# Hybrid streaming encoder step: second part of each weight tile by accumulating DMA instead of GpSimd, and its products after all those with first parts

## The chip, the core and the metric

The kernel runs on one core of a Trainium2 chip. The core has TensorE (PE in the profile; its weight loads are the row PEld), VectorE (DVE), ScalarE (ACT), GpSimd (POOL) and SyncE (SP), each with its own queue of instructions that run in order, and 16 DMA engines. Engines wait for each other through semaphores. The metric is the device time of one execution in microseconds (us); lower is better.

## The reference, cut to what matters

One layer of a hybrid encoder runs over 512 prompt tokens and 64 sample tokens (576 columns together):

```python
shift, scale, gate = split(silu(c) @ W_ada + b_ada, 3)
h = rmsnorm(x, norm_w) * (1 + scale) + shift
proj = h @ W_in                                  # 2048 -> 18032 columns
y_a = (gated RMSNorm of gated_delta_rule(conv(qkv))) @ W_bA   # 16 heads, chunks of 64
y_b = (sparse_attention(top-k of indexer scores) * silu(z)) @ W_bB
x = x + gate * ((sigmoid(ga) * y_a + sigmoid(gb) * y_b) @ W_out)
return final_rmsnorm(x), new caches, new states
```

The four large products (W_in, W_bA, W_bB, W_out) fill most of the time. All data are float32.

## The kernel before, in words

**The main stream.** The weights are cut into 189 tiles of 128 output columns (2048 x 128, held as 128 partitions x 2048 elements, 1 MB): 141 of W_in and 16 each of W_bA, W_bB and W_out. A tile multiplies the 576 columns of activations in two halves of 288. TensorE multiplies in float32r, which keeps fewer bits than float32, so each operand is split in two: for weights, `whi` is the tile rounded to float32r (ACT, a copy) and `wlo` is tile minus `whi` (GpSimd, a subtraction); activations are split in the same way (`hh` and `hl`; later `ga`, `gb`, `mg`). For each of 16 blocks of rows, `half` (line 285) issues three products: whi x high, whi x low, wlo x high. That makes 48 products per half and 96 per tile.

**Buffers.** The raw tile `wraw`, `whi` and `wlo` have two buffers each. While tile n is multiplied, `run_tile` (line 301) has tile n+1 split in four quarters of 128 x 512, one after each of products 4, 14, 24 and 34 of the first half (`split`, line 273), and has tile n+3 loaded after product 10 of the second half, product 58 of the tile (`load`, line 261, from SP). That load goes into the raw buffer of tile n+1, so it waits until that tile is split. Each half of the result has a PSUM bank out of three (`pm`), read by an epilogue (`epi`) on ACT and DVE as soon as the half ends.

**Order of the rest.** Convolutions, delta rule (a chain per head: convolution, decays `e`, products `kk` and `kq`, a triangular solve by the steps `Mt` and `M` on DVE, small DMAs through DRAM, the scan `px`, `pS`, `po`), indexer, top-k and attention are tasks: generators whose steps are put between the products when a rough clock in the kernel (`Plan`, lines 67 to 203) says that their inputs are there. The clock knows fixed costs for each engine's instructions and nothing of what else happens on the chip. The queues of all engines are written in that order, so an engine that comes late makes those that wait for it stand still with all that is queued behind. `join` (line 162) and `drain` emit what is left of a task without products around it.

**Stages.** Up to about 140 us the modulation weights `wa` stream in and the first two tiles are multiplied as `h` appears (`start`, with its own splits); then the indexer, and from about 450 to 1800 us the 16 heads of the delta rule; attention until about 2430 us; then the branch and output products until the end, with little else beside them. Most instructions of DVE, ACT and GpSimd are recorded by one helper, line 55, so the profile is read by tile names.

Of the kernel before, what the change touches and what calls it, by code (L numbers as in the profile page):

```python
# [7 lines left out]
F32 = mybir.dt.float32  # L8
# [9 lines left out]
KO = 16  # L18
# [16 lines left out]
def chunk(c):  # L35
    """a chunk's tokens: their number, where they begin in a sequence with the sample's history, and in one without"""
    return (128, 128 * c, 128 * c) if c < 4 else (TS, TP + 3, TP)


def by_chunk(x):  # L40
    """the prompt's chunks of a [128, 576] tile"""
    return x[:, :TP].rearrange("p (a b) -> p a b", b=128)


class Eng:
    """an engine whose instructions are also put on the plan's clock"""
# [20 lines left out]
class Plan:  # L67
    """Emission order: a main stream of matrix products, and tasks (generators) whose steps are
    emitted between its instructions when, by a rough clock, their inputs are there."""
# [92 lines left out]
    def join(self, *ts):  # L162
        """emit the rest of these tasks (and what else is due meanwhile)"""
        while any(not t.done for t in ts):
            due = min(t.due for t in self.tasks)
            if due > self.pe:
                self.pe = due
            self.tick()


# [1 line left out]
    def bank(self, pool, key, n, name, count=1):  # L172
        """PSUM banks, when the readers of what was in them should be through"""
        while True:
            u = self.banks.setdefault(key, [])
            at = max([0.0] + [self.last.get(x, 0.0) for x in u[-n:][:count]]) if len(u) >= n else 0.0
            if at <= self.pe:
                break
            yield at - self.pe
        t = [pool.tile([128, 512], F32, tag=key, name=f"{name}_{x}") for x in range(count)]  # L180
        u += [x.name for x in t]
        return t[0] if count == 1 else t
# [23 lines left out]
class Kern(Plan):  # L206
# [29 lines left out]
    def rsqrt(self, pool, x, shape, tag):  # L236
        """1/sqrt(x): bit-level start, then three Newton steps."""
        V = self.V
        v = pool.tile(shape, I32, tag=tag + "v", name=tag + "v")
        t = pool.tile(shape, F32, tag=tag + "t", name=tag + "t")  # L240
        V.tensor_scalar(v, x.bitcast(I32), 1, None, op0=ALU.logical_shift_right)
        V.tensor_scalar(v, v, -1.0, 1597463007.0, op0=ALU.mult, op1=ALU.add)
        y = v.bitcast(F32)
        for _ in range(3):
            V.tensor_tensor(t, y, y, op=ALU.mult)
            V.scalar_tensor_tensor(t, t, -0.5, x, op0=ALU.mult, op1=ALU.mult)
            V.scalar_tensor_tensor(y, t, 1.5, y, op0=ALU.add, op1=ALU.mult)
        return y
# [24 lines left out]
    def split(self, n, q, of=4, eng=None):  # L273
        if n >= len(self.stream):
            return
        d = self.stream[n]
        if q == 0:
            d["hi"] = self.wp.tile([128, 2048], F32R, tag="whi", name=f"whi{n}")
            d["lo"] = self.wp.tile([128, 2048], F32R, tag="wlo", name=f"wlo{n}")
        w = KO * d["m"] // of  # L280
        s = slice(w * q, w * q + w)
        self.A.activation(d["hi"][:, s], d["raw"][:, s], AF.Copy)
        (eng or self.G).tensor_tensor(d["lo"][:, s], d["raw"][:, s], d["hi"][:, s].bitcast(F32), op=ALU.subtract)

    def half(self, n, s, ps, ks, hook=None):
# [7 lines left out]
        for k in ks:  # L293
            for w, x in ((hi, ah), (hi, al), (lo, ah)):
                self.mm(ps[:m, :288], w[:, k, :], x[:, k, sl], start=k == 0 and i % 3 == 0, stop=k == KO - 1 and i % 3 == 2)
                i += 1
                if hook:
                    hook(i)
                self.tick()

    def run_tile(self, n):
# [4 lines left out]
        def hook0(i):  # L306
            if i in (4, 14, 24, 34):
                self.split(n + 1, (i - 4) // 10)

        def hook1(i):  # L310
            if i == 10:
                self.load(n + 3)

        for s in range(2):
            ps = self.pm.tile([128, 512], F32, tag="mm", name=f"mm{n}_{s}")
            self.half(n, s, ps, range(KO), hook1 if s else hook0)
            d["epi"](ps, s)

    def run_last(self, n):
        """the last two tiles, the first halves of both before the second ones"""  # L320
        hook = lambda i: self.split(n + 1, (i - 4) // 10) if i in (4, 14, 24, 34) else None
        for s in range(2):
            for t in (n, n + 1):
                ps = self.pm.tile([128, 512], F32, tag="mm", name=f"mm{t}_{s}")
                self.half(t, s, ps, range(KO), hook if (t, s) == (n, 0) else None)
                self.stream[t]["epi"](ps, s)

# [31 lines left out]
    def now(self, gen):  # L359
        """run a generator that needs no waiting for"""  # L360
# [25 lines left out]
    def small_vectors(self, pool, rows):  # L386
# [6 lines left out]
        # half of the taps' weights: silu(y) = (tanh(y/2) + 1) * (y/2)  # L393
# [10 lines left out]
    def c_vectors(self, pool, cr):  # L404
# [9 lines left out]
        # as stationary operands of a quarter of the array's columns  # L414
# [8 lines left out]
    def start(self, ctx, hctx):  # L423
        """shift and scale, h = modulated norm of x by feature, both in two f32r parts, as the weights
        of the modulation stream in; and the first products as h appears"""
# [7 lines left out]
        with tc.tile_pool(name="x0", bufs=2, side="right", reuse_waits="tile") as xp:  # L433
# [4 lines left out]
            def load(m):  # L438
                """two chunks of the weights"""
# [10 lines left out]
            for t in range(5):  # L450
                # the sample's tokens twice, for the halves of the features
# [45 lines left out]
            def fin(g, w):  # L497
                """the sums as [128, 4, 2 (prompt, sample)], with the bias"""
# [65 lines left out]
            def chunks():  # L564
                """the waiting chunks, each on its columns of the array"""
# [71 lines left out]
    def misc(self):  # L637
# [3 lines left out]
        # the indexer's keys in two parts, on both halves of the partitions: prompt, past, sample  # L641
# [21 lines left out]
        # indexer weights by token; for the sample also on the upper partitions  # L663
# [4 lines left out]
        # beta, g, and sums of g along the chunks  # L668
# [16 lines left out]
        # log1p(e) = e * ln(u) / (u - 1) with u = 1 + e rounded; e where u == 1  # L685
# [95 lines left out]
    def qi_epi(self, m):  # L781
        def epi(ps, s):
# [4 lines left out]
            # two heads in two parts, a part on either half of the partitions  # L787
# [64 lines left out]
    def topk(self, a, k, name):  # L852
        """the k largest of each row become MARK (of equal values the first), then the row a mask"""
# [78 lines left out]
    def tokens(self, st, nm, src, s):  # L932
        """src by token, times a scalar per token"""
# [17 lines left out]
    def decays(self, st):  # L951
        """between the tokens of a chunk, for both orientations"""
# [24 lines left out]
    def within(self, name, k, x, dst):  # L977
        """products of k with x inside the chunks, times dst"""
# [10 lines left out]
    def front_k(self, st):  # L989
# [4 lines left out]
        # |k|^2 is the diagonal  # L994
# [23 lines left out]
    def front_q(self, st):  # L1018
# [16 lines left out]
        # q with the decay from the chunk's start, and the chunks' whole decays  # L1035
# [8 lines left out]
    def solve(self, st):  # L1044
        """inverses of the chunks' unit lower triangles I - N (transposed): of the 32 x 32 blocks on their
        diagonals a system per partition, then products for the blocks below of twice the size"""
# [45 lines left out]
        # the 32 x 32 blocks, those of the first halves also not transposed  # L1092
# [20 lines left out]
        # the 64 x 64 blocks  # L1113
# [17 lines left out]
    def scan(self, st):  # L1131
# [46 lines left out]
        # norm over the head, back to features, its weight (and the half of silu(z))  # L1178
# [50 lines left out]
    def bias_setup(self):  # L1229
        """the relative bias of each head by distance, in DRAM; its far value by partition"""  # L1230
# [17 lines left out]
        # every row repeated: a row stride one short of the period then shifts by one per partition  # L1248
# [3 lines left out]
    def toeplitz(self, h, n, w):  # L1252
        """[n, w]: bias at distance c - 128 - p"""
# [47 lines left out]
    def attend_block(self, a, t, BT):  # L1301
        """128 of the prompt's queries of a head"""
# [28 lines left out]
    def softmax(self, L, mask, name, tag):  # L1331
        """L + mask to probabilities along the rows"""
# [89 lines left out]
    def silu2(self, ps, s, dst):  # L1422
        """2 silu of a PSUM half into its part of dst [128, 576]"""
# [37 lines left out]
    def gate_vectors(self):  # L1461
        """half of the third part of silu(c) @ w_ada + b_ada: sums along k by partition, then over partitions"""
# [141 lines left out]
    def out_cols(self, j, g, ts):  # L1604
        """the columns of x plus the output product, their squares' sums, and then times the final weight"""
# [24 lines left out]
    def finish(self, ts, *after):  # L1630
        """the final norm of some rows; the last columns still lack the weight"""
# [189 lines left out]
def shape_constants():  # L1821
    """arrays that depend on shapes alone: identity, chunk triangles, masks, relative-position buckets"""
# [53 lines left out]
```

## Time and profile before

| | |
|---|---|
| Times of three runs | 3176.89, 3191.1, 3197.2 us; median 3191.1 us |
| Profiled execution: span from first to last instruction | 3196.7 us (no other time of it is given; 5.6 us over the median) |
| PE busy | 3018.8 us (94%) |
| DVE, ACT, POOL busy | 1687.6 (53%), 1074.6 (34%), 1098.7 us (34%) |
| DMA | 355.20 MB, queue q1 of SP busy 39.1% of 16 engines' span |

A busy share says how long an engine had an instruction in work, not that it advanced: an instruction that is held up while it runs counts as busy. PEclk is the clock that TensorE was granted as a share of 2.4 GHz; its two levels are 1.0 and 0.5 (1.2 GHz). The DMA share is the mean busy share of the 16 DMA engines.

### The profile page before, as it was taken

What the parts mean: (1) busy time and instruction counts of PE and PEld (TensorE: products, weight loads), DVE (VectorE), ACT (ScalarE), POOL (GpSimd) and SP (SyncE); (2) the same over time, 40 slices, a digit from 0 to 9 for tenths busy, and PEclk for the clock granted to TensorE, in tenths of its full rate; (3) what the DMA queues carried; (4) which work ended last, traced back from release to release, by engine and by line L of the source; (5) the groups of instructions that cost most, each with busy time, mean ns of one, the idle gap of its engine ahead of it and who ended that gap; (6) DMA issues with size and microseconds to landing.
All of it is one profiled execution on the core that took longest, in us unless ns stands there. A gap on an engine that the chain in (4) does not pass through costs nothing.

```text
span 3196.7 us, 55681 instructions
## 1 busy us (share of the span) xinstructions
PE 3018.8 (94%) x22363; PEld 2852.4 (89%) x22363; DVE 1687.6 (53%) x4057; ACT 1074.6 (34%) x2580; POOL 1098.7 (34%) x1103
## 2 busy tenths in 40 slices
PE   6999999999999999999999989999999999999998
PEld 2688999888888888888888879999999999999997
DVE  3355998767678777777776245445442311122112
ACT  2244222343433433334333233323333322122333
POOL 2033343333333333333323323333323434444432
PEclk8999999999999999899989999999999999999999
DMA  9722333322323232232223543343334755444522
GB/s 357 229 56 60 107 98 84 89 79 76 86 77 97 80 87 66 69 89 79 75 71 93 122 121 108 95 138 107 95 100 120 202 166 154 128 136 133 152 80 86
DMA packets 513092, 355.20 MB, mean 111 GB/s; under 512 B 47489, under 2 KB 460050, under 8 KB 511618
## 3 DMA queue, kind: packets, MB, share of 16 engines
q1 hardware_dynamic: 512690, 351.58, 39.1%
q8 instruction: 176, 2.88, 0.4%
q14 instruction: 82, 0.67, 0.1%
q10 hardware_dynamic: 144, 0.07, 0.0%
HBM read 303.54 MB, written 48.04 MB: 110 GB/s over the span
## 4 chain that ended last, share of the span: by engine, by line
PE 68%; DVE 23%; DMA 3%; ACT 2%; issue 2%; SPq 1%; POOL 1%; DVEq 0%; ACTq 0%; POOLq 0%
PE mm L218 55%; DVE Mt L55 5%; DVE M L55 4%; DVE cv L55 3%; DVE L L55 2%; PE dot L218 1%; SPq L55 1%; PE ada L218 1%; PE ob L218 1%; PE lg L218 1%; PE mmp L218 1%; DVE rkt L55 1%; DMA wa<-in_w_ada 1%; POOL wlo L55 1%; DVE e L55 1%
## 5 line engine op out<-in xcount | busy, mean ns | idle before, releaser
L55 POOL TENSOR_TENSOR wlo<-wraw,whi 128x512 fp32r<-128x512 f32 x752 | 1028.3, 1388 | 2006.0 <-ACT whi L55 1898.6
L218 PE MATMUL mm<-hl,whi 128*128 128x288 f32 (+1 forms) x4448 | 1359.6, 306 | 0.0
L218 PE MATMUL mm<-hh,wlo 128*128 128x288 f32 (+1 forms) x4448 | 1356.0, 305 | 0.0
L218 PE MATMUL mm<-hh,whi 128*128 128x288 f32 (+1 forms) x4448 | 1349.2, 303 | 0.3 <-ACT kvTk L55 0.3
L218 PEld LDWEIGHTS mm<-hh,wlo 128*128 128x128 f32 (+1 forms) x4448 | 855.8, 192 | 14.9 <-issue 8.6
L218 PEld LDWEIGHTS mm<-hl,whi 128*128 128x128 f32 (+1 forms) x4448 | 855.4, 192 | 12.6 <-issue 6.2
L218 PEld LDWEIGHTS mm<-hh,whi 128*128 128x128 f32 (+1 forms) x4448 | 855.8, 192 | 9.3 <-issue 4.9
L55 ACT ACTIVATE whi<-wraw 128x512 fp32r<-128x512 f32 x756 | 433.7, 620 | 297.1 <-issue 205.2
L55 DVE TENSOR_TENSOR Mt<-M 18x30 f32<-18x30 f32 (+14 forms) x480 | 220.8, 460 | 9.1 <-issue 0.3
L55 DVE TENSOR_TENSOR M<-M,Mt 18x30 f32<-18x30 f32 (+14 forms) x480 | 205.1, 427 | 16.5
L218 PE MATMUL mm<-mg,whi 128*128 128x288 f32 x1024 | 204.5, 295 | 0.0
L218 PE MATMUL mm<-gb,whi 128*128 128x288 f32 x1024 | 204.0, 296 | 0.0
L218 PE MATMUL mm<-ga,whi 128*128 128x288 f32 x1024 | 203.5, 294 | 0.0
L218 PEld LDWEIGHTS mm<-mg,whi 128*128 128x128 f32 x1024 | 164.0, 188 | 0.0
L218 PEld LDWEIGHTS mm<-ga,whi 128*128 128x128 f32 x1024 | 164.0, 188 | 0.0
L55 DVE SCALAR_TENSOR_TENSOR cv<-raw,cw,cv 128x579 f32<-128x579 f32 x144 | 154.5, 1073 | 17.7 <-ACT cv L55 14.7
L218 PEld LDWEIGHTS mm<-gb,whi 128*128 128x128 f32 x1024 | 163.5, 188 | 0.0
L218 PE MATMUL mm<-mg,wlo 128*128 128x288 f32 x512 | 152.0, 297 | 0.0
L218 PE MATMUL mm<-ga,wlo 128*128 128x288 f32 x512 | 150.8, 295 | 0.0
L218 PE MATMUL mm<-gb,wlo 128*128 128x288 f32 x512 | 150.4, 294 | 0.0
L55 DVE SCALAR_TENSOR_TENSOR gacc<-gada,cs,gacc 128x512 f32<-128x512 f32 x120 | 107.7, 914 | 19.3 <-DMA gada<-in_w_ada 19.3
L55 DVE SCALAR_TENSOR_TENSOR ta<-ta,mm 128x288 f32<-128x288 f32 x32 | 14.5, 454 | 164.8 <-PE mm L218 164.7
(475 smaller groups left out, 3371.0 us busy)
## 6 DMA issues: line engine op xcount, KB each, us to landing
wraw<-in_w_in SPq DMA_DIRECT2D x140, 1024.0 KB
wa<-in_w_ada SPq DMA_DIRECT2D x64, 512.0 KB
gada<-in_w_ada SPq DMA_DIRECT2D x64, 256.0 KB
wraw<-in_w_branch_a SPq DMA_DIRECT2D x16, 1024.0 KB
wraw<-in_w_branch_b SPq DMA_DIRECT2D x16, 1024.0 KB
wraw<-in_w_out SPq DMA_DIRECT2D x16, 1024.0 KB
d_t<-gth SPq DMA_DIRECT2D x32, 288.0 KB
gB<-d_g SPq DMA_DIRECT2D x16, 289.5 KB
```

Source lines behind the costliest of these rows:

```text
L55: r = f(*a, **k)
L218: self.nc.tensor.matmul(out, lhsT, rhs, start=start, stop=stop, **k)
```

## The change

`split` no longer calls GpSimd's subtraction. ACT writes `whi` as before, and then `wlo = -whi`; after every second quarter a DMA of 128 x 1024 elements (0.5 MB), issued from GpSimd's queue, adds `wraw` into `wlo` on the way. The split of one tile in `start`, which names DVE as its engine, is as it was. `half` gets a `part`: 0 for the 32 products of a half with `whi`, 1 for the 16 with `wlo`. `run_tile` issues part 0 of both halves (64 products), then part 1 of the first half, its epilogue, part 1 of the second half and its epilogue. So both halves' PSUM banks are held together. The load of tile n+3 comes after product 84 of the tile instead of 58. `run_last` splits after products 4, 12, 20 and 28. In `start` the products keep the old order. The diff also drops comments and docstrings, which is left out here.

```diff
@@ split
-        (eng or self.G).tensor_tensor(d["lo"][:, s], d["raw"][:, s], d["hi"][:, s].bitcast(F32), op=ALU.subtract)
+        if eng:
+            eng.tensor_tensor(d["lo"][:, s], d["raw"][:, s], d["hi"][:, s].bitcast(F32), op=ALU.subtract)
+            return
+        self.A.activation(d["lo"][:, s], d["hi"][:, s].bitcast(F32), AF.Copy, scale=-1.0)
+        if q % 2:
+            s = slice(w * q - w, w * q + w)
+            self.G.dma_start(d["lo"][:, s], d["raw"][:, s], accum_op=ALU.add)
@@ half
-            for w, x in ((hi, ah), (hi, al), (lo, ah)):
-                self.mm(ps[:m, :288], w[:, k, :], x[:, k, sl], start=k == 0 and i % 3 == 0, stop=k == KO - 1 and i % 3 == 2)
+            for j, (w, x) in enumerate(((hi, ah), (hi, al), (lo, ah))):
+                if part is not None and part != j // 2:
+                    continue
+                self.mm(ps[:m, :288], w[:, k, :], x[:, k, sl], start=k == 0 and j == 0, stop=k == KO - 1 and j == 2)
@@ run_tile
-        def hook0(i):
+        count = [0]
+        def hook(_):
+            i = count[0] = count[0] + 1
             if i in (4, 14, 24, 34):
                 self.split(n + 1, (i - 4) // 10)
-        def hook1(i):
-            if i == 10:
+            if i == 84:
                 self.load(n + 3)
-        for s in range(2):
-            ps = self.pm.tile([128, 512], F32, tag="mm", name=f"mm{n}_{s}")
-            self.half(n, s, ps, range(KO), hook1 if s else hook0)
-            d["epi"](ps, s)
+        ps = {}
+        for part in range(2):
+            for s in range(2):
+                if not part:
+                    ps[s] = self.pm.tile([128, 512], F32, tag="mm", name=f"mm{n}_{s}")
+                self.half(n, s, ps[s], range(KO), hook, part)
+                if part:
+                    d["epi"](ps[s], s)
```

**ACT's queue at tile 170** (a tile of W_bB; numbers behind the names count tiles and buffers; `waits` names the semaphores of engines, PE_49 of TensorE, and of DMAs, DMAHW from SP and DMASW from GpSimd). Before:

```order
L55 ACTIVATE whi170_30321<-wraw170_30150 128x512 [waits DMAHW7_49,PE_49,Pool_49]
L55 ACTIVATE mg0_28871<-tb11_30192 128x576 [waits DMAHW0_49,DVE_49]
L55 ACTIVATE whi170_30321<-wraw170_30150 128x512 x3
L55 ACTIVATE whi171_30441<-wraw171_30270 128x512 [waits DMAHW2_49,PE_49,Pool_49]
```

With the change:

```order
L55 ACTIVATE whi170_30659<-wraw170_30512 128x512 [waits DMAHW7_49,PE_49]
L55 ACTIVATE wlo170_30660<-whi170_30659 128x512 [waits DMASW6_49,DMASW7_49,PE_49,Activation_49]
L55 ACTIVATE mg0_29185<-tb11_30528 128x576 [waits DMAHW0_49,DVE_49]
L55 ACTIVATE whi170_30659<-wraw170_30512 128x512
L55 ACTIVATE wlo170_30660<-whi170_30659 128x512 [waits Activation_49]
```

ACT has two instructions per quarter where it had one, and the second waits for the first.

**GpSimd's and SP's queues at the same tile.** Before, GpSimd and then SP's load of a later tile (SP's last row of each piece):

```order
L55 TENSOR_TENSOR wlo170_30322<-wraw170_30150,whi170_30321 128x512 [waits DMAHW7_49,PE_49,Activation_49]
L55 TENSOR_TENSOR wlo170_30322<-wraw170_30150,whi170_30321 128x512 [waits Activation_49] x3
L55 DMA wraw172_30390<-in_w_branch_b 128x16x128 [waits DMAHW7_49,Pool_49]
```

With the change:

```order
L55 DMA wlo170_30660<-wraw170_30512 128x1024 [waits DMASW7_49,DMASW6_49,DMAHW7_49,PE_49,Activation_49]
L55 DMA wlo170_30660<-wraw170_30512 128x1024 [waits Activation_49]
L55 DMA wraw172_30756<-in_w_branch_b 128x16x128 [waits DMASW3_49,DMAHW7_49,DMASW2_49,Activation_49]
```

Four subtractions have become two DMAs, and the load that waited for GpSimd (Pool) now waits for two DMAs of GpSimd's queue (DMASW).

**TensorE's queue at the end of head 15's scan**, where `px153` and `pS153` are its last step, `oTp15` turns its normed result, and the stage drains behind it (`mm94` is tile 94, the last before the drain). Before, rows of products stand between them, one by one, 76 products from `px153` to `oTp15`; the last rows:

```order
L218 MATMUL mm94_1_19185<-hl_100,whi94_18926 128x288
L218 MATMUL mm94_1_19185<-hh_99,wlo94_18927 128x288
L233 MATMUL oTp15_0_19261<-ident_60,ot15_18940 128x128 x4
L233 MATMUL oTq15_0_19267<-ident_60,ot15_18940 128x64
L218 MATMUL mm95_0_19276<-hh_99,whi95_19103 128x288
```

With the change there are 27 (the sum of the counts x9, x2 and x16):

```order
L218 MATMUL px153_0_19376<-r153_19368,TT15_18204 128x128
L218 MATMUL mm94_0_19259<-hh_99,wlo94_19082 128x288 x9
L218 MATMUL pS153_0_19389<-x153_19378,kd15_18641 128x128
L218 MATMUL po153_19364<-x153_19378,e115_18124 128x128
L218 MATMUL mm94_0_19259<-hh_99,wlo94_19082 128x288 x2
L218 MATMUL mm94_1_19312<-hh_99,wlo94_19082 128x288 x16
L233 MATMUL oTp15_0_19452<-ident_60,ot15_19173 128x128 x4
```

The step before the drain comes 49 products later in the stream; products with `wlo` now stand together at a tile's end.

## Rows read from the trace of the kernel before

**Rows 1.** Windows: stretch, its length, busy us (instructions) per engine, PEclk, DMA share, GB/s.

```profile
0.00:100.00 100.00, 71.88 (x374) 31.38 (x374) 34.79 (x78) 22.52 (x62) 19.32 (x20) 0.91 0.96 342
...
400.00:1700.00 1300.00, 1203.25 (x9269) 1149.54 (x9268) 994.10 (x2468) 484.19 (x1167) 462.93 (x620) 0.95 0.31 81
...
2500.00:2700.00 200.00, 200.00 (x1511) 200.00 (x1510) 45.14 (x73) 55.34 (x106) 83.09 (x63) 1.00 0.59 174
2700.00:2900.00 200.00, 200.00 (x1509) 200.00 (x1509) 34.27 (x63) 41.99 (x74) 85.60 (x64) 1.00 0.43 128
2900.00:3000.00 100.00, 100.00 (x758) 100.00 (x757) 20.85 (x37) 26.86 (x64) 41.86 (x31) 1.00 0.56 171
3000.00:3180.00 180.00, 179.81 (x1368) 179.57 (x1367) 27.69 (x72) 63.63 (x224) 62.38 (x50) 1.00 0.27 77
```

**Rows 2.** Chain that ended last (start us, us, what): a tile's products, and the next.

```profile
2982.78 12.74 PE mm L218 x96
...
2996.06 12.72 PE mm L218 x96
```

**Rows 3.** PE's waits: who waited <- for whom, us in total, times, longest.

```profile
PE px L218 <- DVE r L55: 23.5, 18, 3.8
PE kk L218 <- DVE k L55: 22.3, 9, 4.0
...
PE z L218 <- DVE Z L55: 13.7, 9, 2.7
...
PE vbp L233 <- DVE Mt L55: 9.6, 3, 3.2
...
PE vbp L233 <- ACT kd L55: 4.2, 5, 1.0
```

**Rows 4.** Instructions on tiles Mt, M: duration ns min/median/max, first and last start.

```profile
L55 DVE TENSOR_TENSOR Mt<-M x480: 171/344/1497, 475.2 to 1743.0; 18x30 f32<-18x30 f32 x16, 18x108 f32<-18x108 f32 x16, 18x168 f32<-18x168 f32 x16, 18x210 f32<-18x210 f32 x16
L55 DVE TENSOR_TENSOR M<-M,Mt x480: 178/340/1506, 476.5 to 1743.2; 18x30 f32<-18x30 f32 x16, 18x108 f32<-18x108 f32 x16, 18x168 f32<-18x168 f32 x16, 18x210 f32<-18x210 f32 x16
```

**Rows 5.** Instructions on tile cv, the same view.

```profile
L55 DVE SCALAR_TENSOR_TENSOR cv<-raw,cw,cv x144: 802/822/1852, 445.3 to 1718.5; 128x579 f32<-128x579 f32 x144
```

**Rows 6.** Timeline of DVE: start us, us, engine, line, operation.

```profile
1513.40 3.70 DVE L55 TENSOR_SCALAR ssk<-ssk 128x5 f32<-128x5 f32 x1
1517.13 0.17 DVE L55 TENSOR_SCALAR rkv<-ssk 128x5 int32<-128x5 int32 x1
```

**Rows 7.** Timeline of POOL in the same microseconds.

```profile
1513.25 3.74 POOL L55 TENSOR_TENSOR wlo<-wraw,whi 128x512 fp32r<-128x512 f32 x3
```

**Rows 8.** Page, costliest groups: xcount | busy us, mean ns | idle before, releaser.

```profile
L55 POOL TENSOR_TENSOR wlo<-wraw,whi 128x512 fp32r<-128x512 f32 x752 | 1028.3, 1388 | 2006.0 <-ACT whi L55 1898.6
...
L55 ACT ACTIVATE whi<-wraw 128x512 fp32r<-128x512 f32 x756 | 433.7, 620 | 297.1 <-issue 205.2
L55 DVE TENSOR_TENSOR Mt<-M 18x30 f32<-18x30 f32 (+14 forms) x480 | 220.8, 460 | 9.1 <-issue 0.3
L55 DVE TENSOR_TENSOR M<-M,Mt 18x30 f32<-18x30 f32 (+14 forms) x480 | 205.1, 427 | 16.5
...
L55 DVE SCALAR_TENSOR_TENSOR cv<-raw,cw,cv 128x579 f32<-128x579 f32 x144 | 154.5, 1073 | 17.7 <-ACT cv L55 14.7
```

**Rows 9.** Windows, instructions on wlo alone: PE, PEld, DVE, POOL; PEclk, DMA share, GB/s.

```profile
400.00:1700.00 1300.00, 709.51 (x2299) 450.10 (x2299) 0.00 (x0) 401.65 (x288) 0.95 0.31 81
```

**Rows 10.** Page, DMA queues: packets, MB, share of 16 engines' span.

```profile
q1 hardware_dynamic: 512690, 351.58, 39.1%
```

**Rows 11.** Chain that ended last, near 780 us.

```profile
776.88 4.10 POOL wlo L55 x3
...
781.00 5.60 DMA wraw<-in_w_in
786.60 2.11 ACT M L55
```

**Rows 12.** Timeline of ACT: an epilogue's first read of a PSUM bank.

```profile
1012.85 0.41 ACT L55 ACTIVATE gz<-mm 128x288 f32<-128x288 f32 x1 [0.36 <-PE mm L218]
```

**Rows 13.** Timeline of DVE: the same epilogue's last read of that bank.

```profile
1022.18 0.44 DVE L55 SCALAR_TENSOR_TENSOR gz<-gz,mm 128x288 f32<-128x288 f32 x1
```

More of the change, by code (lines that the diff above doesn't have):

```diff
@@ L282, in split, with half @@
         self.A.activation(d["hi"][:, s], d["raw"][:, s], AF.Copy)
-        (eng or self.G).tensor_tensor(d["lo"][:, s], d["raw"][:, s], d["hi"][:, s].bitcast(F32), op=ALU.subtract)
-    def half(self, n, s, ps, ks, hook=None):
+        if eng:
[5 more added lines that the diff above has]
+            self.G.dma_start(d["lo"][:, s], d["raw"][:, s], accum_op=ALU.add)
+    def half(self, n, s, ps, ks, hook=None, part=None):
         d = self.stream[n]
@@ L304, in run_tile @@
             d["pre"]()
-        def hook0(i):
+        count = [0]
+        def hook(_):
+            i = count[0] = count[0] + 1
             if i in (4, 14, 24, 34):
                 self.split(n + 1, (i - 4) // 10)
-        def hook1(i):
-            if i == 10:
+            if i == 84:
                 self.load(n + 3)
-        for s in range(2):
-            ps = self.pm.tile([128, 512], F32, tag="mm", name=f"mm{n}_{s}")
-            self.half(n, s, ps, range(KO), hook1 if s else hook0)
-            d["epi"](ps, s)
+        ps = {}
[6 more added lines that the diff above has]
+                    d["epi"](ps[s], s)
     def run_last(self, n):
-        hook = lambda i: self.split(n + 1, (i - 4) // 10) if i in (4, 14, 24, 34) else None
+        hook = lambda i: self.split(n + 1, (i - 4) // 8) if i in (4, 12, 20, 28) else None
         for s in range(2):
@@ L324, in run_last @@
                 ps = self.pm.tile([128, 512], F32, tag="mm", name=f"mm{t}_{s}")
-                self.half(t, s, ps, range(KO), hook if (t, s) == (n, 0) else None)
+                self.half(t, s, ps, range(KO), hook if (t, s) == (n, 0) else None, 0)
+                self.half(t, s, ps, range(KO), None, 1)
                 self.stream[t]["epi"](ps, s)
```

## The prediction

> **What bounds the kernel now.** I read the windows first. From 2500 us to the end TensorE is busy all the time at the full clock, the 2.4 GHz level [rows 1]; a tile of 96 products takes 12.74 us, 133 ns each, and the next begins 13.28 us after the last [rows 2]. The number of products and of weight loads stays the same, so nothing is to be won there; it can only be lost, if weights come late. The other large stretch is the delta rule, 400 to 1700 us: PE is busy 1203.25 of 1300 us, so 96.75 us stand idle, and the granted clock is 0.95 [rows 1], which means about 65 us of clock lost in stretches at the lower level (a twentieth of 1300).
>
> Second, the list of PE's waits: in that stage it waits for DVE, `r`, `k`, `Z`, `Mt` [rows 3], never for `whi` or `wlo`. So the splitting of weights holds PE up nowhere directly. It does so through DVE. `cv` takes 802 ns at its fastest, 822 in the median and up to 1852; `Mt` and `M` have medians of 344 and 340 ns but maxima of 1.5 us [rows 4, 5]. The timeline shows why: a DVE instruction on 128 x 5 elements took 3.70 us, its neighbour on as many elements 0.17, and it ended as three GpSimd subtractions that had run 3.74 us came to their end [rows 6, 7]. While GpSimd runs `wlo`, DVE stands. That is the cost which the change removes.
>
> **What is removed.** 752 subtractions of 1388 ns, 1028 us of GpSimd [rows 8]; GpSimd's own time is on no path worth naming, the hold on DVE is. Its size, mean less median: `Mt` 480 x (460 - 344) ns = 56 us, `M` 480 x (427 - 340) = 42 us, `cv` 144 x (1073 - 822) = 36 us [rows 4, 5, 8], together 134 us, 8.4 us for each of 16 heads, beside which stand shorter instructions like that of 3.70 us. (The medians of `Mt` mix shapes, so this is an estimate.) The PE idle time is 6.0 us per head (96.75/16). If all DVE lateness came from GpSimd, all 97 us and 65 us of clock would go; if DVE is late for its own work's sake (it is busy 994 of 1300 us, and the plan's clock is rough), nothing goes. I take 65% of the idle time, **63 us**, since the relief per head exceeds the wait per head but lies partly in moments when nobody waits; and half of the clock loss, **33 us**, as the low clock follows the gaps. Together -96 us, bounds 0 and -162.
>
> **What is added.**
> - *ACT*: 752 more copies; their price by the row of `whi`, 620 ns [rows 8], is 466 us, and each waits for the one before it. In the delta stage ACT is busy 484 of 1300 us, 37% [rows 1]; the 288 subtractions there [rows 9] become 288 copies of 0.62 us, 179 us, 51%. PE takes no result of it directly late: the last of four pairs is done about 5 us after a tile begins. But convolution, decays and scan have steps on ACT, some 45 a head, which now stand behind a pair of 1.24 us rather than 0.62. Bounds 0 and 60 us (a fifth of 45 x 16 steps, 0.4 us later); I take **15 us**, near the lower, since PE hardly waits for ACT today.
> - *The accumulating DMAs*: 376 of 524 KB. No row shows one. At the rate of the first window, 342 GB/s at a share of 0.96, one stream of 524 KB takes 1.5 us of all 16 engines; at q1's mean, 351.58 MB in 39.1% of 3196.7 us = 281 GB/s, 1.9 us [rows 1, 10]. The DMA must read both `wraw` and `wlo`, so I count two streams, 3.3 us in the middle; bounds 1.5 (one stream) and 6.0 (three streams at 81 GB/s in a share of 0.31, 261 GB/s, the slowest row [rows 1]). At 3.3 us they fill 39% of the span beside the 39% of today. The last 680 us hold two per 13.28 us, a share of 0.50: with 0.59 and 0.56 [rows 1] that is 1.09 and 1.06, an overflow of 18 + 6 us; those loads run ahead, so I take half, **12 us**; at 1.5 us none. In the opening, where the share is 0.96, four DMAs of 3.3 us land among the modulation weights: 13 us, of which I take **9** (bounds 0 and 24).
> - *Is `wlo` in time?* In the last stage four pairs take about 5 us, GpSimd's issue, which no row shows, is taken as long as a subtraction, 1.4 (0 to 5), the DMA 3.3: ready 9.7 us after a tile begins, wanted 64 products into the next, 13.3 + 8.5 = 21.8. Twelve us of cover; that is what the new order of products buys.
> - *The load of tile n+3*, behind those DMAs in SP's queue: it is issued after product 84, 11.2 us, when the DMAs are done, and lands 5.6 us later [rows 11], 16.8, wanted at 26.6. Nothing, unless the DMAs take over 4 us longer; then SP stands, and small transfers of the solve behind it. The chain of waits shows that this path (split, load, ACT waiting for it) already holds up `M` now and then [rows 11].
> - *PSUM banks*: the first half's bank is wanted again 48 products after its epilogue begins, 6.4 us, where it was 96. DVE's last read came 9.8 us after ACT's first in one case [rows 12, 13]. At worst 3.4 us in each of 16 heads, 54 us; with DVE relieved I take **5**; a gain is excluded, since banks are only held longer.
> - *The drain after head 15*: 76 products stood behind `px153`, now 27; the norm's chain loses a cover of 49 x 0.133 = **6.5 us**.
> - The order of products as such, the other memsets on GpSimd, `run_last`: nothing; the products and their weight loads are the same in number, and the last tile's `wlo` is wanted 80 products after its first split.
>
> Sum: -96 + 15 + 12 + 9 + 5 + 6.5 = -48.5 us on the profiled 3196.7: 3148; the median of the runs lies 5.6 lower, so the forecast is **3142 us**.
>
> Two rules weighed. The timeline shows DVE held while a GpSimd instruction that reads and writes SBUF runs [rows 6, 7]. The Trainium skill, page "SBUF — State Buffer", section "Who interferes with whom", says that a DVE instruction with two SBUF inputs contends with a GpSimd instruction that reads SBUF and not with one that only writes it; by that, GpSimd writing descriptors would not hold `Mt`, `M` and `cv` at all, and the first term would go to its bound, which is rival 3. And for the price of an accumulation, the Trainium skill, page "Collectives: The Full Stack", section on the fold count, says that the addition costs nothing beyond the second read, at 31 GB/s per engine over two reads: by estimate from that page 2.1 us per DMA; the overflow of the last stage would vanish, 3130 us.
>
> **Rivals.**
> 1. *The accumulating DMAs are slow and bind the last stage* (slower). For: the share there is 0.59 and 0.56 already, and no row shows a transfer that adds. Against: rows of 4 KB in SBUF on both sides. At x us each the share there grows by x/6.64. It decides from about 4.0 us, where the overflow (200 x 0.19 + 200 x 0.03 + 100 x 0.16 = 60 us) eats the gain; at 5 us it is 68 + 36 + 31 + 4 = 139 us, and 3142 - 12 + 139 = 3269 us. Chance 0.16.
> 2. *ACT takes GpSimd's place*: the chain of each head, freed on DVE, waits on ACT behind pairs of copies, and on banks. At the upper bounds, 60 + 54 for the 20 in the sum, 3236 us; midway 3189. For: ACT's `M` of 2.11 us and `cv` stand on the chain [rows 11]. Against: of PE's waits for ACT the longest sum is 4.2 us [rows 3]. Chance 0.22, most of it between 3175 and 3215.
> 3. *All lateness of DVE was GpSimd's*: 3196.7 - 162 + 47.5 - 5.6 = 3077 us. For: 8.4 us of relief against 6.0 of idle time per head. Against: the plan's clock is too fast for DVE anyway. Chance 0.12.
> 4. *The hold stays*: GpSimd prepares the transfers itself and holds DVE as long as before; the costs without the gain, 3239 us. Chance 0.04.
>
> **Numbers.** The forecast's case has 0.46 and its own range 3085 to 3180. Beyond 1% of 3191, about what a measurement of this kernel can tell from no change, means under 3159 or over 3223. Faster: 0.8 of 0.46, and rival 3: 0.50. Within: the rest of the forecast's case, most of rival 2: 0.29. Slower: rivals 1 and 4 and the end of 2: 0.21. The range leaves out half of rival 3 below and half of rival 1 above: 3075 to 3250.
>
> **What would show it.** `cv` at a mean near 820 ns and `Mt` near 345; PE's idle time in the delta stage near 35 us and its clock near 0.98; ACT busy near 1540 us, 48%; the accumulating queue at 30 to 45% of the engines; no wait of PE for `wlo`. Wrong if PE in the last stage waits for `wlo` or ACT for `wraw` (rival 1), if PE's waits in the delta stage go from DVE to ACT (rival 2), or if `cv` still reaches 1.8 us (rival 4).

## The result, and the profile after

The changed kernel takes **3103.85 us** (median; 3100.01 to 3106.55 us) against 3191.15 us on the same chip: ratio 0.9732, 95% interval 0.9706 to 0.9758, or 2.7% faster. The forecast was 3142, with a range of 3075 to 3250. The profiled execution spans 3104.8 us, where the one of before spans 3196.7. Times here and below are medians of fast runs; a single run of 4762.57 us, of the kernel with two idle reads below, is left out as slow.

The windows of the kernel after (columns as in [rows 1]: length, busy us and instructions of PE, PEld, DVE, ACT, POOL, granted clock, DMA share, GB/s):

```profile
0.00:100.00 100.00, 67.62 (x315) 27.25 (x315) 30.98 (x75) 27.55 (x70) 11.91 (x16) 0.86 0.98 332
400.00:1700.00 1300.00, 1269.12 (x10184) 1218.95 (x10183) 839.25 (x2629) 722.46 (x1593) 194.18 (x496) 0.98 0.68 156
1700.00:1750.00 50.00, 27.61 (x164) 25.46 (x163) 9.41 (x31) 11.82 (x27) 1.72 (x2) 0.73 0.85 155
2450.00:2600.00 150.00, 143.19 (x1063) 142.28 (x1062) 17.86 (x33) 60.12 (x103) 18.99 (x22) 0.99 0.92 230
2800.00:2900.00 100.00, 93.94 (x710) 93.70 (x709) 16.27 (x33) 38.70 (x74) 11.21 (x13) 1.00 0.94 242
```

The delta-rule stretch now has 30.9 us without PE where it had 96.75, and a clock of 0.98 for 0.95 [rows 1]. DVE is busy 839 us there instead of 994 (by the exact bounds of the stage 778 instead of 988, with the same 2549 instructions: 210 us of hold). Against that, PE has gaps in the last stages, which had none: 6.8 us in 150 and 6.1 in 100, where the DMA share is 0.92 and 0.94. The 50 us after 1700, at a clock of 0.73, hold the opening of attention, which ends at 1718.7.

Two of the tiles in [rows 5] and [rows 6], after (ns min/median/max, first and last start):

```profile
L55 DVE SCALAR_TENSOR_TENSOR cv<-raw,cw,cv x144: 772/821/825, 452.9 to 1586.9; 128x579 f32<-128x579 f32 x144
L55 DVE TENSOR_SCALAR ssk<-ssk x16: 170/172/175, 464.3 to 1558.1; 128x5 f32<-128x5 f32 x16
```

The median of `cv` has not moved; its maximum fell from 1852 ns to 825. That is how a hold looks: the typical instruction is as before, the tail is gone. The groups of the page that answer to [rows 8] (busy us, mean ns, idle before):

```profile
L55 POOL DMA_DIRECT2D wlo<-wraw x376 | 324.3, 863 | 2340.4 <-ACT wlo L55 2062.9
L55 ACT ACTIVATE whi<-wraw 128x512 fp32r<-128x512 f32 x756 | 467.3, 619 | 96.1 <-DMA wraw<-in_w_branch_b 40.2
L55 ACT ACTIVATE wlo<-whi 128x512 fp32r<-128x512 f32 x752 | 475.2, 632 | 70.0 <-PE mm L218 31.6
L55 DVE TENSOR_TENSOR Mt<-M 18x30 f32<-18x30 f32 (+14 forms) x480 | 151.8, 316 | 34.1 <-DMA M<-dN 24.8
L55 DVE SCALAR_TENSOR_TENSOR cv<-raw,cw,cv 128x579 f32<-128x579 f32 x144 | 117.4, 815 | 4.3 <-ACT cv L55 0.8
```

The means of `Mt` and `cv` fell from 460 and 1073 ns to 316 and 815; the page gives DVE 1389.1 us in all. The DMA queues, and the issue of the new transfers (KB, median us to landing):

```profile
q1 hardware_dynamic: 512690, 351.58, 40.1%
q0 software_dynamic: 54144, 197.16, 33.5%
...
wlo<-wraw POOLq DMA_DIRECT2D x376, 512.0 KB, 5.4
```

An accumulating DMA takes 0.335 x 3104.8 / 376 = 2.77 us of all 16 engines. PE's waits over the whole span (us in total, times, longest):

```profile
PE px L218 <- DVE r L55: 13.3, 3, 4.7
...
PE yp L233 <- ACT og L55: 8.0, 2, 7.5
PE mm L218 <- ACT gth L55: 6.4, 3, 4.5
PE mm L218 <- DVE ta L55: 6.4, 3, 4.6
...
PE mm L218 <- DMA wlo<-wraw: 4.9, 1, 4.9
```

Of the waits in [rows 3], 13.3 of 23.5 us for `r` are left. The next three lie in the last stages: epilogues (`gth`, `ta`) that come late and hold a PSUM bank, and an output tile `og` for which its transposition `yp` waits. Before, `yp` is the only one of them, with 0.7 us. The chain of waits shows why (start, us, what):

```profile
2401.13 11.05 DMA za<-d_za
...
2445.06 8.75 DMA d_t<-gth
...
2460.72 9.26 DMA gbl<-d_gb
2470.01 0.69 ACT gb L55
```

These three transfers of under 300 KB take 9 to 11 us among the accumulating ones. ACT stands 6.37 us for `d_t` and 10.67 for `gbl`, and the epilogues behind them are late. `og` is late behind a longer transfer on the same chain, the load of x for the end:

```profile
2870.73 27.04 DMA xf<-in_x_sample
```

ACT's waits for DMAs in the last stages, from 2300 us on, first before and then after:

```profile
ACT gb L55 <- DMA gbl<-d_gb: 17.4, 11, 3.0
```

```profile
ACT gb L55 <- DMA gbl<-d_gb: 78.9, 12, 12.6
ACT whi L55 <- DMA wraw<-in_w_branch_b: 40.2, 8, 10.0
ACT whi L55 <- DMA wraw<-in_w_branch_a: 10.5, 1, 10.5
ACT whi L55 <- DMA wraw<-in_w_out: 9.0, 2, 7.3
```

So weight loads come late too, which they did not before, but PE waits for no `whi` there.

The two traces by stage, from the first PE instruction of a tile to that of the next stage's first tile (us; in time the products on `gb` stand between those on `ga` and on `mg`, and "end" is what follows PE's last instruction):

| stage | before | after | difference |
|---|---|---|---|
| to the first whole tile | 142.3 | 149.5 | +7.2 |
| indexer | 311.3 | 311.2 | -0.1 |
| delta rule (first `kk` to first `kcp`) | 1351.1 | 1222.8 | -128.3 |
| opening of attention (`kcp` to `lg`) | 26.7 | 35.1 | +8.4 |
| attention | 602.8 | 599.2 | -3.7 |
| last gates; products on `ga`; on `mg` | 543.5 | 567.9 | +24.4 |
| products on `gb`; end | 219.0 | 218.9 | -0.1 |

### The profile page after: what moved, and what is told of

The parts are those of the page before. It is cut to its first block, busy times and chain, and to the rows that moved or that the text cites. A ratio compares the mean times of both kernels' runs of the same rounds, so it can differ in the third digit from the quotient of the medians.

```text
span 3104.8 us, 56419 instructions
## 1 busy us (share of the span) xinstructions
PE 2972.8 (96%) x22363; PEld 2816.3 (91%) x22363; DVE 1389.1 (45%) x4057; ACT 1542.5 (50%) x3332; POOL 390.0 (13%) x727
## 3 DMA queue, kind: packets, MB, share of 16 engines
q0 software_dynamic: 54144, 197.16, 33.5%
## 4 chain that ended last, share of the span: by engine, by line
PE 49%; DMA 9%; SPq 3%; ACT 2%; DVE 2%; issue 1%; POOL 0%; ACTq 0%; DVEq 0%; POOLq 0%
PE mm L218 41%; SPq L55 3%; DMA gbl<-d_gb 2%; DMA za<-d_za 2%; DMA wlo<-wraw 2%; PE ob L218 1%; PE lg L218 1%; DMA xf<-in_x_sample 1%; ACT wlo L55 1%; ACT whi L55 1%; PE po L218 1%; PE pT L233 1%; PE obs L218 1%; PE lgs L218 0%; DVE M L55 0%
## 5 line engine op out<-in xcount | busy, mean ns | idle before, releaser
L218 PE MATMUL mm<-hh,whi 128*128 128x288 f32 (+1 forms) x4448 | 1222.3, 301 | 6.1 <-ACT gth L55 5.8
L218 PE MATMUL mm<-hl,whi 128*128 128x288 f32 (+1 forms) x4448 | 1219.8, 300 | 0.0
L218 PE MATMUL mm<-hh,wlo 128*128 128x288 f32 (+1 forms) x4448 | 685.0, 303 | 4.9 <-DMA wlo<-wraw 4.9
L218 PEld LDWEIGHTS mm<-hh,wlo 128*128 128x128 f32 (+1 forms) x4448 | 619.5, 191 | 13.2 <-DMA wlo<-wraw 5.1
L55 POOL DMA_DIRECT2D wlo<-wraw x376 | 324.3, 863 | 2340.4 <-ACT wlo L55 2062.9
L55 ACT ACTIVATE wlo<-whi 128x512 fp32r<-128x512 f32 x752 | 475.2, 632 | 70.0 <-PE mm L218 31.6
L55 DVE TENSOR_TENSOR Mt<-M 18x30 f32<-18x30 f32 (+14 forms) x480 | 151.8, 316 | 34.1 <-DMA M<-dN 24.8
L218 PE MATMUL mm<-ga,whi 128*128 128x288 f32 x1024 | 141.1, 297 | 7.1 <-DVE ta L55 6.4
L218 PE MATMUL mm<-mg,whi 128*128 128x288 f32 x1024 | 144.3, 298 | 0.0
L218 PE MATMUL mm<-gb,whi 128*128 128x288 f32 x1024 | 138.1, 294 | 0.0
```

The costliest lines, as they stand in the source:

```text
L55: r = f(*a, **k)
L218: self.nc.tensor.matmul(out, lhsT, rhs, start=start, stop=stop, **k)
```

## The experiments

The theory: the gain is the end of the hold, since GpSimd instructions that read SBUF stop DVE, and an accumulating DMA does not. Its rival: the gain comes from the new order of products and loads. Each ratio is to the kernel before on the same chip; kernels of different chips are best compared by their ratios.

**The order alone.** The changed kernel with this in `split`, in short:

```
-  ACT lo = -hi;  every second quarter: G.dma_start(lo, raw, accum_op=add)
+  G.tensor_tensor(lo, raw, hi, op=subtract)
```

> The changed order of products, load and epilogues, but GpSimd still subtracts (no accumulating DMA, no second copy on ACT). Theory (DVE was held by GpSimd's reading instructions): DVE is held as before, cv mean near 1070 ns, delta stage near 1350 us, plus some 6 us for the drain behind head 15: 3190 to 3205 us. Rival (the new order gives the gain): delta stage near 1225 us, and without the costs of the DMAs about 3070 to 3105 us.

3180.01 us, ratio 0.9964 (0.9943 to 0.9985): about 11 us of the gain (5 to 18). That is 10 us below the theory's range and 75 above the rival's. The delta stage takes 1338 us; `cv` is held as before:

```profile
L55 DVE SCALAR_TENSOR_TENSOR cv<-raw,cw,cv x144: 776/822/1856, 442.3 to 1700.9; 128x579 f32<-128x579 f32 x144
```

So the order by itself is not the gain. Nor does it cost the 6 us expected of it: the opening of attention behind the drain takes 24.4 us (before: 26.7), and start and last stages are no longer than they were. (The trace is of this kernel's quickest run, 3170.65 us.)

**The split alone.** The kernel before, with ACT's second copy and the accumulating DMA in `split`, and nothing else.

> The new split (ACT writes -hi, a DMA adds the raw weights) in the old order of products, where the third product of a tile already reads the second part. Theory (hold): the delta stage falls to about 1225 us all the same; each wlo is there some 13 us after the tile before begins and wanted at 13.5 us and, its second half, at 19.7 us, so PE waits now and then for it: 3085 to 3130 us. Rival (the order gives the gain): 3190 us or more, delta stage near 1350 us. If the order is what keeps the DMAs off PE's path, waits of PE for wlo sum to over 50 us.

3212.21 us, ratio 1.0059 (1.0041 to 1.0077), **slower than before**, outside the theory's range and where its rival had the time (3190 us or more). But the rival's reason, a delta stage near 1350 us, does not show. The hold is gone (`cv` 826 ns at most, DVE 1392.4 us), yet the delta stage only falls to 1295 us, and PE has two new waits, the first in the delta stage; SP's queue, in 480 to 1700 us, has the third row:

```profile
PE z L218 <- DMA TT<-dX: 52.5, 28, 5.9
PE mm L218 <- DMA wlo<-wraw: 46.2, 20, 12.1
```

```profile
SPq L55 <- DMA wlo<-wraw: 576.2, 63, 18.0
```

As the waits of the load in SP's queue say, the load of a raw tile cannot be issued before the accumulating DMA has read the slot's last tile; SP stands there, and the solve's small transfers (`dX` to `TT`) stand behind it. So neither half of the change is a gain of this size alone. Two runs take the order apart.

**The load back at product 58**, new order of products:

```
-            if i == 84:
+            if i == 58:
                 self.load(n + 3)
```

> The changed kernel with the load of tile n+3 issued after product 58 again, as before, not after product 84; the new order of products stays. Theory (the load stands in SP's queue until the accumulating DMA has read the raw tile, and the small transfers of the solve stand behind it): waits of z for the solve's DMAs rise from 3 to over 30 us, the delta stage from 1223 to 1260 to 1300 us, total 3135 to 3180 us. Rival (what the order buys is only the 64 products of cover for wlo): 3104 us, no wait of z for DMA.

3199.56 us, ratio 1.0032 (1.0015 to 1.005), 96 us slower than the changed kernel and above my range. The delta stage takes 1299 us; the last gates and the products on `ga` are 23 us longer too. PE's wait, then SP's in 480 to 1700 us:

```profile
PE z L218 <- DMA TT<-dX: 55.3, 28, 5.9
```

```profile
SPq L55 <- DMA wlo<-wraw: 621.2, 58, 18.6
```

In the changed kernel, the same two views say:

```profile
PE z L218 <- DMA TT<-dX: 3.0, 7, 0.8
```

```profile
SPq L55 <- DMA wlo<-wraw: 378.0, 51, 14.7
```

SP stands much even there, but PE hardly ever waits behind it.

**The old order of products with the load at product 84**: `split_alone` with `if i == 10` of the second half turned into `if i == 36`.

> The new split in the old order of products, with only the load moved to product 84. Theory (two separate debts: the late load frees SP's queue, the order of products covers wlo): the delta stage falls near 1225 to 1250 us, while PE still waits some 46 us for wlo, 3 us of it in the delta stage and the rest in the opening of attention and behind it: 3140 to 3175 us. Rival (one debt: the products' order alone): 3205 to 3215 us as with the load at product 58.

3143.14 us, ratio 0.9856 (0.9831 to 0.988); delta stage 1242 us, as two debts predict:

```profile
PE mm L218 <- DMA wlo<-wraw: 37.2, 17, 12.2
PE z L218 <- DMA TT<-dX: 26.4, 22, 4.2
```

The four kernels with accumulating DMAs side by side (us):

| | load at product 58 | load at product 84 |
|---|---|---|
| first and second parts mixed | 3212 | 3143 |
| second parts last | 3200 | 3104 |

The late load is worth 69 to 96 us, the order of products 13 to 39. Each is worth more with the other.

**The hold given back.** The changed kernel, with idle GpSimd work in the delta stage, behind each quarter's split, on a scratch tile of 128x256 (`idle`). Three forms:

```
+  two times:    G.tensor_tensor(idle, idle, idle, op=add)
+  four times:   G.memset(idle, 0)
+  three times:  G.tensor_scalar(idle, idle, 1.0, op0=mult)
```

> The changed kernel, and in the delta stage, behind each quarter's split, two idle GpSimd instructions of 128x256 that read two SBUF operands and write one (own scratch, nobody reads it): about the GpSimd time of the subtraction removed. Theory (hold): DVE is held again, cv mean near 1000 to 1100 ns, delta stage from 1223 back to 1320 to 1360 us, total 3200 to 3240 us. Rivals (order of products, or the subtraction's place in the chain of splits): cv 815 ns, delta stage 1223 us, total 3104 us.

> As the kernel with idle GpSimd instructions, but these only write: four memsets of 128x256 per quarter, some 1.2 us, in the delta stage. Theory with the skill's rule (only a GpSimd instruction that reads SBUF holds DVE's two-operand instructions): cv 815 ns, delta stage 1223 us, total 3104 us. Rival (GpSimd's busy time as such holds DVE, or its queue delays somebody): cv 1000 ns or more, delta stage 1320 us or more, total 3200 us or more.

> As the kernel with idle GpSimd instructions of two reads, but three instructions of 128x256 per quarter that read one SBUF operand and write one. Theory with the skill's rule (any read of SBUF by GpSimd holds DVE's two-operand instructions): DVE held in proportion to GpSimd's busy time, delta stage over 1280 us, total over 3160 us. Rival (only the two-operand form holds): delta stage 1223 us, total 3104 us.

By tiles, `cv` and then GpSimd's instruction (ns min/median/max). Two reads:

```profile
L55 DVE SCALAR_TENSOR_TENSOR cv<-raw,cw,cv x144: 772/822/1704, 452.4 to 1684.3; 128x579 f32<-128x579 f32 x144
```

```profile
L55 POOL TENSOR_TENSOR idle<-idle x648: 602/627/1927, 358.9 to 1752.9; 128x256 f32<-128x256 f32 x162
```

Writes only:

```profile
L55 DVE SCALAR_TENSOR_TENSOR cv<-raw,cw,cv x144: 773/821/825, 452.0 to 1608.1; 128x579 f32<-128x579 f32 x144
```

```profile
L55 POOL MEMSET idle<- x1296: 302/313/776, 358.6 to 1674.7; 128x256 f32 x186
```

One read:

```profile
L55 DVE SCALAR_TENSOR_TENSOR cv<-raw,cw,cv x144: 772/831/1073, 457.1 to 1679.8; 128x579 f32<-128x579 f32 x144
```

```profile
L55 POOL TENSOR_SCALAR idle<-idle x972: 842/852/2369, 360.4 to 1755.7; 128x256 f32<-128x256 f32 x195
```

| idle GpSimd work | GpSimd busy, added | DVE busy, added | delta stage | time | ratio (95%) |
|---|---|---|---|---|---|
| none (the changed kernel) | 0 | 0 | 1222.8 | 3103.85 | 0.9732 |
| two reads | 449 | 173 | 1322.6 | 3207.29 | 1.0049 (1.003 to 1.0069) |
| writes only | 398 | 9 | 1245.1 | 3129.68 | 0.9816 (0.9784 to 0.9847) |
| one read | 894 | 77 | 1319.5 | 3207.84 | 1.0053 (1.0038 to 1.0067) |

The run with two reads is in the theory's range, though `cv` has a mean of 949 ns, less than the 1000 to 1100 expected; that with writes only is 26 us above it. For about the same GpSimd time, two reads cost 103 us and writes 26. The memsets hold no two-input instruction of DVE (`cv` at most 825 ns). Their 26 us are, as far as the waits tell, queueing: the issue of the accumulating DMA stands behind them, SP stands longer for its end, and PE waits 23.9 us for `TT`, where it was 3.0. The first run pays no more for its queue: SP's wait in 480 to 1700 us is the same with two reads and with writes only (378.0 without idle work),

```profile
SPq L55 <- DMA wlo<-wraw: 473.9, 60, 18.5
```

```profile
SPq L55 <- DMA wlo<-wraw: 473.5, 61, 16.3
```

and PE waits 14.2 us for `TT` there. So some 77 us are left for the reading. The run with one read is in the range of its theory, but not by its mechanism: DVE is held far less, and not in proportion to GpSimd's busy time (77 us for 894, where two reads held it 173 for 449; `cv` at most 1073 ns), but GpSimd is so full that the DMAs come late (34.8 us of waits for `TT`). It does not price a single read.

**DVE subtracts**, in the new order: no GpSimd subtraction, no accumulating DMA, no second copy.

```
-        if eng:
-            eng.tensor_tensor(...subtract)
+        if True:
+            (eng or self.V).tensor_tensor(...subtract)
```

> The changed order, but DVE subtracts: no GpSimd instruction of any size, no accumulating DMA, no second copy on ACT. DVE gets 752 subtractions of 0.7 us (620 ns for 448 columns in the kernel before), 526 us, 202 us of them in the delta stage (DVE there 839 + 202 of 1223 us). Theory (what mattered was the hold, 282 us of DVE time, 215 in the delta stage, in pieces of up to 3.7 us): about as much DVE time as the hold took, but in pieces of 0.7 us; the delta stage between 1223 and 1350, near 1290 us, and the 24 us of the late stages and 7 us of the start are not paid: 3120 to 3170 us. If DVE's time in sum decides and not the pieces: 3190 us or more.

3142.82 us, ratio 0.9846 (0.9831 to 0.9861), within the theory's range; the delta stage of 1310 us is longer than the 1290 expected. (By the pages the hold took 298 us of DVE time, 210 of them in the stage, not 282 and 215.) In that stage DVE is busy 974 us, against 979 with the order alone, where the hold takes as much as the subtractions do here; and the stage is 28 us shorter. That fits the theory that the sum of DVE's time decides most of it, and the length of the pieces less, but it does not show it, since PE waits elsewhere. With the order alone its waits are spread over `Z` (24.3 us), `r` (16.0), `S` (13.7) and `k` (9.7); here nearly all of them are one, behind the scale `fs` of a head's norm, and DVE stands for `whi` as well (PE's, ACT's and DVE's waits in 453 to 1763 us):

```profile
PE oTp L233 <- ACT ot L55: 68.4, 11, 8.4
```

```profile
ACT ot L55 <- DVE fs L55: 68.4, 16, 5.7
```

```profile
DVE wlo L55 <- ACT whi L55: 40.4, 41, 2.8
```

**ACT's second copy done twice:**

```
+        self.A.activation(d["lo"][:, s], d["hi"][:, s].bitcast(F32), AF.Copy, scale=-1.0)   # once more
```

> The changed kernel with each -hi copy done twice: 752 more copies of 0.62 us on ACT, 466 us, ACT busy near 2005 us. Theory (ACT lies under PE's work; the first 752 copies cost next to nothing): 3104 to 3115 us, the few us from the DMAs that start 0.6 us later. Rival (ACT's copies cost what the prediction counted, 15 us, up to 60): 3119 to 3165 us, PE waiting for ACT in the delta stage.

3311.75 us, ratio 1.0383 (1.0346 to 1.0419): **both theories miss**, by 147 us and more. ACT is busy 1997.8 us. PE's waits in 460 to 1850 us:

```profile
PE oTp L233 <- ACT ot L55: 44.7, 9, 6.7
PE z L218 <- DMA TT<-dX: 26.0, 15, 3.9
```

The delta stage is 142 us longer than in the changed kernel, attention 32, the products on `ga` 22. A second copy also delays each accumulating DMA by up to 2.5 us a tile, so I can't part ACT's own queue from the later transfers. The run does show that the changed kernel stands close to an edge.

**Accumulating DMAs in fewer places.** GpSimd subtracts again from `open_ga` on; then for the first two tiles as well; then everywhere but in the delta stage:

```
-        if eng:
+        if eng or self.late:          # late: set in open_ga; third kernel: False only from open_gdn to open_att
-            eng.tensor_tensor(...)
+            (eng or self.G).tensor_tensor(...)
...
+                    self.split((n - 32) // 8, (n - 32) // 2 % 4, 4, G)     # second kernel: the start
```

> The changed kernel, but from the last gates of branch a on (tile products on W_bA, the gates of b, W_bB, W_out) GpSimd subtracts again; accumulating DMAs only up to there. Theory (the late stages lose 24 us to the crowded DMA engines; DVE there is not what PE waits for): 3104 - 24, 3075 to 3090 us, all of it in the stages after attention. Rival (the loss comes from the order of products or the banks): 3100 to 3108 us.

> As the kernel with GpSimd subtracting in the late stages, and the first two tiles, split among the modulation weights, by GpSimd as well. Theory (the four accumulating DMAs there cost the start 7 us): 7 us less than with the late stages alone, 3068 to 3083 us, start of the first tile as in the kernel before. Rival (the start's 7 us is the order or run-to-run scatter): no difference.

> The new order everywhere, but accumulating DMAs in the delta-rule stage alone; GpSimd subtracts in the start, the indexer stage, attention and all behind it. Theory (DVE's hold matters in the delta stage only; DMAs elsewhere only crowd the engines, 8 us in the opening of attention too): 3065 - 8, 3050 to 3062 us. Rival (attention gains from the free DVE as well): 3062 to 3080 us.

| accumulating DMAs | us | ratio (95%) | what the traces say |
|---|---|---|---|
| everywhere | 3103.85 | 0.9732 (0.9706 to 0.9758) | |
| not in the late stages | 3079.05 | 0.9654 (0.9638 to 0.967) | last gates, `ga`, `mg`: 567.9 to 540.0 us |
| nor in the start | 3065.0 | 0.9607 (0.9591 to 0.9622) | first tile at 140.0 us, was 148.1 |
| in the delta stage alone | **3052.4** | 0.9575 (0.955 to 0.9599) | opening of attention 24.4 us, was 35.8 |

The steps gave 25, 14 and 13 us (expected 24, 7 and 8). The second is 3 us below its range, and only 8 us of it lie at the start, the rest in stages that are the same in both kernels; by the ratios the third is 10 us. The last kernel is the best of all, 51 us below the changed one. Outside the delta stage DVE is held again there, 106 us in all (1495.4 us busy for 1389.1), and attention is not longer for it (596.7 us for 599.2). Its windows:

```profile
0.00:100.00 100.00, 72.56 (x379) 31.88 (x379) 33.81 (x78) 22.52 (x62) 19.34 (x20) 0.91 0.96 343
400.00:1700.00 1300.00, 1268.89 (x10202) 1218.46 (x10200) 833.91 (x2621) 719.23 (x1589) 205.04 (x502) 0.99 0.69 156
2450.00:2600.00 150.00, 150.00 (x1134) 150.00 (x1133) 27.52 (x35) 34.26 (x60) 62.35 (x47) 1.00 0.52 154
```

The delta stage keeps all of its gain; PE is busy without a gap in the last stages, where GpSimd subtracts as before the change.

## Why the prediction was right, and where its sizes were off

- **The mechanism was right.** The forecast named the hold on DVE as what the change removes, and the place where it counts. It shows as predicted: `cv` at a mean of 815 ns (820 forecast), `Mt` at 316 (345), PE's idle time in the stage 30.9 us (35), clock 0.98 (0.98), ACT 1542.5 us busy (1540), the accumulating queue 33.5% (30 to 45).
- **The gain was too small, by the clock term and the order.** In the same 1300 us the idle time fell by 65.9 us (96.75 to 30.9), 68% where 65% was forecast; in the whole stage of 1351 us it fell by 73 (103.7 to 30.9). The clock term was 33, half of the loss; at the granted clock 70.0 us were lost in the whole stage before, and 22.1 after, so 48, two thirds of it. The stage gained 128 us net of what ACT and banks may cost, where -96 was forecast and -162 was the bound. Of these 128, 13 came with the order alone, which was counted at nothing. The truth lies between the forecast and rival 3.
- **ACT, +15, and PSUM banks, +5**: too much, as far as the trace shows. In the delta stage PE waits for ACT once, 3.7 us, and for no bank. But the bound of 60 us rested on too little; the next 455 us of copies, and the later DMAs behind them, cost 208 us. Rival 2 had a cliff behind it that the average load of 51% does not show.
- **The price of the DMA, 3.3 us**: 2.77 measured, nearer to the two streams counted than to either bound. By the page "Collectives: The Full Stack" of the Trainium skill, section on the fold count, it was 2.1 by estimate; the measurement lies between. The loss in the last stages that this estimate would have made vanish did come, though not as an overflow (next point).
- **The late stages, +12**: 24 in the stages, 25 by the run without the DMAs there. The step that failed is "those loads run ahead, so I take half". It treated the share over 1 as a delay of weight loads alone. They did come late: ACT waits 59.7 us for `wraw`, a sign that was named for rival 1, but PE waits there neither for `whi` nor for `wlo`, and 2.77 us are below the 4.0 from which rival 1 was to decide. What PE waits behind are small transfers for the next activations and the load of x, at shares of 0.88 to 0.94, below 1. How much of the epilogues' lateness comes from ACT's standing for `wraw` is not parted; without the accumulating DMAs there, both are gone from PE's waits (0.5 us left).
- **The start, +9**: 8 us by the first tile's time.
- **The drain after head 15, +6.5**: wrong. With the order alone the opening of attention costs nothing more, and the whole kernel is 11 us faster, where drain and banks were to cost 11.5. The 8 us that the changed kernel loses there come from the accumulating DMAs, since the kernel with them in the delta stage alone has them back; I had no term for that place.
- **`wlo` in time, the load nothing**: right. PE waits for `wlo` once, 4.9 us, in that opening. The sentence that SP would stand with the small transfers of the solve behind it, if the DMAs took longer, named the very path that opens when the load stays at product 58. What the prediction didn't say is how much hung on it: 96 us.
- **The rule on who is held.** In the runs with idle work two-read instructions of GpSimd hold `cv`, memsets do not. The Trainium skill, page "SBUF — State Buffer", section "Who interferes with whom", has DVE's two-input instructions contend with a GpSimd instruction that reads SBUF and not with one that only writes; these two runs agree (1704 ns and 825 ns at most). It is not the whole of the hold: `ssk` of [rows 6], held for 3.70 us, has one input. And beside the memsets, which leave two-input instructions alone (0.6 us more in sum), DVE's one-input `tensor_scalar`s take 9.3 us more in sum, `ssk` up to 387 ns where it was 175. GpSimd's preparing of the transfers, 863 ns each, does not hold `cv` (825 ns at most), so rival 4 fails.

The sum was right in sign. On the profiled executions it was 43 us too high: the idle and clock terms 32 us too small, ACT, banks and drain counted at 26.5 and not seen, start and attention 6 better, the late stages and the opening of attention 21 worse.

## What to carry to other kernels

Look for a hold by comparing median and maximum of one instruction: where the median is clean and the tail is long, try moving the other engine's work off the shared path. Here 201 us less of DVE time in the delta stage (979 to 778 from the order alone to the whole change) gave back 115 us of it, as PE's idle time and its lost clock fell together. A transfer that replaces compute needs a place in three queues: give it time before its consumer, and move whatever waits for its end (here a load on SP) behind that end. Use it in the stage where the engine that it relieves is waited for; elsewhere, in this kernel, it only crowded the transfers.

## What was not expected of the hardware

- A GpSimd instruction on 128x256 takes 627 ns with two inputs (tensor_tensor, median), 852 with one input and a scalar (tensor_scalar), 313 as a memset. The form with fewer operands was the slower one.
- The hold seems to go both ways: GpSimd's own instructions stretch to 1927 ns (from 627) and 2369 ns (from 852) in the two runs with reads, and memsets to 776 (from 313). Spans on GpSimd are rough, and no run parts this from other causes.
- An accumulating DMA from SBUF to SBUF moves its 4096-byte packets in 339 ns (median of 48,128), where a plain packet of 2048 bytes on SP's queue takes 84: four times the time for twice the bytes.
